# One decoder layer on one core: which weight granules the DMA queue splits, the order of the attention half of the output projection, and the division of SBUF between weight buffers and general slots

## The chip, the cores and the metric

The kernel runs on one core of a Trainium2 chip. The core has five engines, each with an instruction queue that is worked off in order: TensorE (PE; its weight loads are shown as PEld), VectorE (DVE), ScalarE (ACT), GpSimd (POOL) and SyncE (SP). SP and POOL also issue the transfers between HBM and SBUF. The metric is the device time of one execution in microseconds (us); lower is better.

## The reference

One layer works on x of 512 positions by 1024 channels, in float32. What matters here:

```python
h = rms_norm(x, norm1_g[l])
proj = h @ w_in[l]
z, xbc, dt, q, kv, gates = jnp.split(proj, split_points, axis=-1)
y_ssm = ssd_mixer(z, xbc, dt, ...)
y_nsa = rms_norm(nsa_mixer(q, kv, gates, ...), attn_norm_g[l])
x = x + jnp.concatenate([y_ssm, y_nsa], axis=-1) @ w_out[l]
h = rms_norm(x, norm2_g[l])
u = causal_dwconv(h @ ffn_w_up[l], ffn_conv_w[l], ffn_conv_b[l])
ug, uv = jnp.split(u, 2, axis=-1)
x = x + (jax.nn.silu(ug) * uv) @ ffn_w_down[l]
return rms_norm(x, final_norm_g)
```

`ssd_mixer` is a state-space scan in four chunks of 128 positions. `nsa_mixer` is an attention with a compressed, a selected and a windowed branch; the compressed branch first makes 31 compressed keys and values out of windows of 32 positions.

## The kernel before

**Products in three parts.** Every large product is made of three matmuls: each operand is split into a rounded part (high) and the rest (low), and high by high, high by low and low by high are added in one PSUM bank. So each weight granule (128 partitions by 1024 columns, 512 KB) is needed as `wh` (high) and `wl` (low).

**Two ways to split a granule.** The 144 granules are consumed in a fixed sequence `seq`: 0 to 39 of w_in, 40 to 55 of w_out (40 to 47 for the attention half, 48 to 55 for the scan half), then the feed-forward part. `by_dma(i)` picks the way. By the engines: two transfers of 256 KB from SP's queue into slots `wr`, then for each half ACT (or DVE, as CAST) writes `wh`, and DVE or POOL subtracts to make `wl`. By DMA: POOL issues one transfer of 512 KB into `wh`, ACT writes its negated rounded value into `wl`, and POOL issues a second transfer of the same 512 KB that adds the granule onto `wl`; the granule is thus read from HBM twice, and neither DVE nor POOL computes.

**Look-ahead and buffers.** `w_get(i, ahead)` hands out granule i and records the splits of the following ones (two, or three when the next is split by DMA) and the loads of two more (LOOK). There are 7 buffers `wh` and 7 `wl`; all other tiles of 2 KB a partition share 53 slots.

**The planner sets the order.** The program is first recorded and then placed by `schedule`, a list scheduler with its own costs: at each step the engine that can start earliest takes the ready operation that was recorded first. It also picks the engine (ACT or DVE, DVE or POOL) and the buffer. The order of every engine's queue is therefore an outcome of the recorded order, of the costs (among them the rate it assumes for a transfer, 360, or 180 for an adding one) and of the free buffers.

**The stages on PE, in order.** `first_job` (granules 0 to 3, tiles `psa`, while the norm's row sums are made: `n1ss`, `n1rb`, then hT, the normalised and transposed input, in `hTh` and `hTl`); the compressed branch's projections (4 to 7, `psb`), whose results are copied by SP transfers into shifted tiles `x2a` and `x2b`, gathered into `cxb` by ACT and DVE and multiplied in `compress` (tile `cps`); keys, queries and the scan's inputs (8 to 39) woven with the attention (`pss`, `tb`, `o`); then the scan `ssd` woven with `out_nsa` (40 to 47, tiles `on`); `out_ssm` (48 to 55, tiles `os`); the second norm (`n2`, `tb`) and the feed-forward part (`psb`, `dn`).

**out_nsa before.** For each half of the 1024 output columns it fetches its four granules at once, loads x again into `xr`, and then takes one block of 128 positions (t) after the other: 24 matmuls over all four granules into one bank `on`, then a DVE operation that scales the bank and adds it to `xr`. `out_ssm` goes t by t over four granules in the same way.

Of the kernel before, what the change touches and what calls it, by code (L numbers as in the profile page):

```python
# [15 lines left out]
ALU = mybir.AluOpType  # L16
# [5 lines left out]
NT = 4  # L22
# [1 line left out]
KC = 8  # L24
FF = 2816
NEG = -1.0e30
N_SLOT = 53
N_WH = 7
N_WL = 7
AHEAD = 3  # L30
LOOK = 2
D0, D1 = 8, 56
N_EAGER = 3
HEADS = (4, 2, 1, 1)
N_WARM = 10
# [133 lines left out]
class Program:  # L169
# [82 lines left out]
    def _cost(self, op, e, n, args, kw, ins, outs):  # L252
# [12 lines left out]
            return ins[0].free / 1.2 + (52 if is_ps[0] else 94) + 93 * extra, TABLE.get(args[2].name, 0)  # L265
        if n == "dma_start" and e == "POOL":
            v = outs[0]
            op.lat = v.ids.shape[0] * v.free * 4 / (180.0 if "accum_op" in kw else 360.0)
            return 1000.0, 0
        if e in ("DVE", "POOL"):  # L270
            f = max([v.free for v in ins] + [outs[0].free])
# [14 lines left out]
                op.port[e] = e == "POOL" or sb > 1 or (sb == len(big) == 1 and not is_ps[0] and n not in ("reciprocal", "tensor_reduce"))  # L286
            return cost * (2.0 if e == "POOL" else 1.0), 0
        v = (outs + ins)[0]
        op.lat = v.ids.shape[0] * v.free * 4 / 360.0
        return 650.0, 0  # L290


# [119 lines left out]
def layer_kernel(ctx: ExitStack, tc: tile.TileContext, x, xt, win, wdtg, wout, wup, wdn, pack, gcol, rows, cw1, consts, rot, out):  # L412
# [20 lines left out]
    def bank(name, shape=(P, T)):  # L433
        return alloc(pp, shape, F32, name, "b", 8)
# [238 lines left out]
    RS = {}  # L673
# [524 lines left out]
    def nsa_root(h):  # L1198
        ps = bank("oss", (P, 2, 2))
        for t in range(2):  # L1200
            for p_ in range(2):
                mm(ps[:, t], ACC[h][:, p_, t], ones[:, 0:2], start=p_ == 0, stop=p_ == 1)
        r = rstd_of(ps[:, :, 0], 2, 1024, 1e-6, "nsa")
        for t in range(2):
            RS["nsa", 2 * h + t] = r[:, t:t + 1]
# [47 lines left out]
    def nxt(n=1):  # L1253
        g = gi[0]
        gi[0] += n
        return g
# [124 lines left out]
    X1 = {}  # L1381

    def out_nsa(half):
        if half == 0:
            for h in range(2):
                for g in range(4):
                    if g >= N_EAGER:
                        nsa_ops(g, h)
                nsa_root(h)
        for t in range(NT):  # L1390
            X1[t, half] = slot(f"xr{t}")
            SP.dma_start(X1[t, half], x[t * P:(t + 1) * P, half * 512:(half + 1) * 512])
        g0 = nxt(4)
        ws = [w_get(g0 + p_, 3 - p_) for p_ in range(4)]
        for t in range(NT):
            ps = bank(f"on{t}")
            for p_ in range(4):
                for j in range(2):
                    tri(ps, mix(t, 2 * p_ + j), [a[:, j * 512:(j + 1) * 512] for a in ws[p_]],
                        p_ == 0 and j == 0, p_ == 3 and j == 1)  # L1400
                yield 1.3
            V.scalar_tensor_tensor(X1[t, half], ps, RS["nsa", t], X1[t, half], op0=ALU.mult, op1=ALU.add)

    def out_ssm(half):
        g0 = nxt(4)
# [205 lines left out]
```

## Time and profile before

| | |
|---|---|
| time, median of 3 runs | 919.08 us (918.53 to 921.29) |
| the profiled execution: time, and its span from first to last instruction | 917.42 us, 915.6 us |
| PE busy in the span | 883.9 us (97%) |
| DVE busy | 682.8 us (75%) |
| ACT busy | 433.0 us (47%) |
| POOL busy | 111.0 us (12%) |
| bytes moved by transfers | 106.02 MB |
| granted TensorE clock, mean | 0.994 |

Busy is the time in which an engine had an instruction running; matmuls overlap each other, so a busy PE is not PE at its peak. A matmul of 512 columns shows a duration of some 390 ns, yet follows the one ahead of it after 0.23 us when nothing is waited for. All times below are counted from the start of the span.

### The profile page before, as it was taken

What the parts mean: (1) busy time and instruction counts of PE and PEld (TensorE: products, weight loads), DVE (VectorE), ACT (ScalarE), POOL (GpSimd) and SP (SyncE); (2) the same over time, 40 slices, a digit from 0 to 9 for tenths busy, and PEclk for the clock granted to TensorE, in tenths of its full rate; (3) what the DMA queues carried; (4) which work ended last, traced back from release to release, by engine and by line L of the source; (5) the groups of instructions that cost most, each with busy time, mean ns of one, the idle gap of its engine ahead of it and who ended that gap; (6) DMA issues with size and microseconds to landing.
All of it is one profiled execution on the core that took longest, in us unless ns stands there. A gap on an engine that the chain in (4) does not pass through costs nothing.

```text
span 915.6 us, 13236 instructions
## 1 busy us (share of the span) xinstructions
PE 883.9 (97%) x4621; PEld 727.6 (79%) x4621; DVE 682.8 (75%) x1466; ACT 433.0 (47%) x939; POOL 111.0 (12%) x138
## 2 busy tenths in 40 slices
PE   8998999999999999999999999999999999999996
PEld 5776777787887799888777779888888888888885
DVE  6956899998889876689898477777773347777535
ACT  5624577787676666578665244222321113222113
POOL 0331231111111111102322221000000000000000
PEclk9999999999999999999999999999999999999999
DMA  8798754454454454432859922111112661000002
GB/s 274 222 223 204 168 119 96 95 121 106 103 127 93 93 105 103 93 116 48 209 165 304 332 83 93 54 50 47 47 58 98 227 226 35 1 0 1 1 1 92
DMA packets 45217, 106.02 MB, mean 116 GB/s; under 512 B 5984, under 2 KB 6752, under 8 KB 45152
## 3 DMA queue, kind: packets, MB, share of 16 engines
q0 software_dynamic: 13824, 50.34, 24.6%
q1 hardware_dynamic: 31328, 54.86, 18.3%
q8 instruction: 36, 0.59, 0.3%
q14 instruction: 29, 0.24, 0.1%
HBM read 97.31 MB, written 2.10 MB: 109 GB/s over the span
## 4 chain that ended last, share of the span: by engine, by line
PE 74%; DVE 10%; DMA 6%; issue 6%; ACT 2%; POOL 2%; SPq 1%; POOLq 0%; DVEq 0%; ACTq 0%
PE psb L400 36%; PE dn L400 13%; PE psa L400 8%; PE pss L400 5%; PE tb L400 4%; PE o L400 4%; PE os L400 2%; DMA rw<-rx 1%; DMA x2b<-rx 1%; PE on L400 1%; DVE hTl L400 1%; DMA wl<-in_wout_dram 1%; DMA x2b<-vcr 1%; SPq L400 1%; DMA wr<-in_win_dram 1%
## 5 line engine op out<-in xcount | busy, mean ns | idle before, releaser
L400 PE MATMUL psb<-hTh,wh 128*128 128x512 f32 (+1 forms) x600 | 232.8, 390 | 2.5 <-ACT cup L400 1.0
L400 PE MATMUL psb<-hTl,wh 128*128 128x512 f32 (+1 forms) x600 | 230.4, 384 | 2.3 <-DVE hTl L400 2.3
L400 PE MATMUL psb<-hTh,wl 128*128 128x512 f32 (+1 forms) x600 | 230.0, 384 | 0.0
L400 ACT ACTIVATE wh<-wr 128x512 fp32r<-128x512 f32 x80 | 49.8, 631 | 202.0 <-PE psb L400 102.1
L400 PEld LDWEIGHTS psb<-hTh,wh 128*128 128x128 f32 x600 | 113.2, 189 | 23.7 <-ACT cup L400 1.5
L400 PEld LDWEIGHTS psb<-hTl,wh 128*128 128x128 f32 x600 | 113.3, 189 | 23.5 <-DVE hTl L400 3.6
L400 PEld LDWEIGHTS psb<-hTh,wl 128*128 128x128 f32 x600 | 113.2, 189 | 21.6
L400 DVE TENSOR_TENSOR wl<-wr,wh 128x512 fp32r<-128x512 f32 x133 | 90.2, 714 | 17.1 <-ACT wh L400 16.8
L400 DVE CAST wh<-wr 128x512 fp32r<-128x512 f32 x68 | 28.9, 426 | 91.9 <-PE psb L400 43.7
L400 ACT ACTIVATE p<-pss,nm 128x128 f32<-128x128 f32 (+3 forms) x128 | 66.8, 525 | 38.0 <-DVE nm L400 21.3
L400 PE MATMUL dn<-wh,gTh 128*128 128x512 f32 (+1 forms) x186 | 70.3, 378 | 0.0
L400 PE MATMUL dn<-wl,gTh 128*128 128x512 f32 (+1 forms) x186 | 70.3, 378 | 0.0
L400 PE MATMUL dn<-wh,gTl 128*128 128x512 f32 (+1 forms) x186 | 70.2, 378 | 0.0
L400 DVE TENSOR_TENSOR ptl<-tb,pth 128x512 fp32r<-128x512 f32 x80 | 54.3, 687 | 14.6 <-ACT pth L400 11.0
L400 ACT ACTIVATE wl<-wh 128x1024 fp32r<-128x1024 f32 x48 | 50.6, 1056 | 27.7 <-DMA wh<-in_wout_dram 14.9
L400 DVE TENSOR_REDUCE nm<-pss 128x1 f32<-128x384 f32 (+3 forms) x88 | 55.5, 633 | 4.0 <-PE pss L400 3.4
L400 PE MATMUL tb<-ck,p 128*128 128x128 f32 x320 | 51.4, 275 | 1.4 <-DVE p L400 1.0
L400 POOL TENSOR_TENSOR wl<-wr,wh 128x512 fp32r<-128x512 f32 x15 | 21.0, 1410 | 225.6 <-ACT wh L400 206.2
L400 ACT ACTIVATE pth<-tb 128x512 fp32r<-128x512 f32 x62 | 36.9, 598 | 21.9 <-PE tb L400 16.4
L400 POOL DMA_DIRECT2D wl<-in_win_dram x32 | 28.2, 882 | 150.4 <-ACT wl L400 136.3
L400 PEld LDWEIGHTS tb<-ck,p 128*128 128x128 f32 x320 | 37.5, 140 | 8.8 <-DVE p L400 1.2
L400 PEld LDWEIGHTS dn<-wh,gTh 128*128 128x128 f32 x186 | 35.0, 188 | 6.7 <-DVE xr L400 0.2
(325 smaller groups left out, 1739.2 us busy)
## 6 DMA issues: line engine op xcount, KB each, us to landing
wr<-in_wup_dram SPq DMA_DIRECT2D x88, 256.0 KB, 4.3
wh<-in_win_dram POOLq DMA_DIRECT2D x32, 512.0 KB, 4.1
wl<-in_win_dram POOLq DMA_DIRECT2D x32, 512.0 KB, 5.4
wr<-in_wdn_dram SPq DMA_DIRECT2D x44, 256.0 KB, 3.4
wh<-in_wout_dram POOLq DMA_DIRECT2D x16, 512.0 KB, 5.3
wl<-in_wout_dram POOLq DMA_DIRECT2D x16, 512.0 KB, 7.5
wr<-in_win_dram SPq DMA_DIRECT2D x16, 256.0 KB, 7.0
rw<-rx SPq DMA_DIRECT2D x56, 64.0 KB, 3.8
```

The costliest lines, as they stand in the source:

```text
L400: getattr(engines[op.eng], name)(*[real(a) for a in args], **{k: real(v) for k, v in kw.items()})
```

## The change

Four things change. The granules split by DMA are 16 to 47 instead of 8 to 55: granules 8 to 15 and 48 to 55 now go through `wr` and are split by the engines. There are 5 buffers `wh` and 5 `wl` instead of 7 and 7, and 61 slots instead of 53 (the same SBUF in all). `out_nsa` takes granule by granule: each granule's six matmuls for each of the four t go into four banks that stay open over the four granules, x is loaded again after that in the recorded order, and the four banks are read at the end. And the planner assumes lower transfer rates (290 and 145).

```diff
-N_SLOT = 53
-N_WH = 7
-N_WL = 7
+N_SLOT = 61
+N_WH = 5
+N_WL = 5
 AHEAD = 3
 LOOK = 2
-D0, D1 = 8, 56
+D0, D1 = 16, 48
...
-            op.lat = v.ids.shape[0] * v.free * 4 / (180.0 if "accum_op" in kw else 360.0)
+            op.lat = v.ids.shape[0] * v.free * 4 / (145.0 if "accum_op" in kw else 290.0)
...
-        op.lat = v.ids.shape[0] * v.free * 4 / 360.0
+        op.lat = v.ids.shape[0] * v.free * 4 / 290.0
...
+        ps = [bank(f"on{t}") for t in range(NT)]
+        g0 = nxt(4)
+        for p_ in range(4):
+            w = w_get(g0 + p_)
+            for t in range(NT):
+                for j in range(2):
+                    tri(ps[t], mix(t, 2 * p_ + j), [a[:, j * 512:(j + 1) * 512] for a in w],
+                        p_ == 0 and j == 0, p_ == 3 and j == 1)
+                yield 1.3
         for t in range(NT):
             X1[t, half] = slot(f"xr{t}")
             SP.dma_start(X1[t, half], x[t * P:(t + 1) * P, half * 512:(half + 1) * 512])
-        g0 = nxt(4)
-        ws = [w_get(g0 + p_, 3 - p_) for p_ in range(4)]
         for t in range(NT):
-            ps = bank(f"on{t}")
-            for p_ in range(4):
-                for j in range(2):
-                    tri(ps, mix(t, 2 * p_ + j), [a[:, j * 512:(j + 1) * 512] for a in ws[p_]],
-                        p_ == 0 and j == 0, p_ == 3 and j == 1)
-                yield 1.3
-            V.scalar_tensor_tensor(X1[t, half], ps, RS["nsa", t], X1[t, half], op0=ALU.mult, op1=ALU.add)
+            V.scalar_tensor_tensor(X1[t, half], ps[t], RS["nsa", t], X1[t, half], op0=ALU.mult, op1=ALU.add)
```

Since the planner decides, the order moves at many places. Three of them bear on what follows.

PE, before, at the end of `first_job` (`n1rb` spreads the norm's factor over the partitions, `psa` are the first granules' products, `psb` the first product that needs hT):

```order
L400 MATMUL n1rb_384<-ck_128,n1r_363 128x128 x4
L400 MATMUL psa_130<-wh3_231,xgh_238 128x512
L400 MATMUL psa_134<-wh3_231,xgh_238 128x512
L400 MATMUL psa_119<-wl3_253,xgh_238 128x512
L400 MATMUL psa_123<-wl3_253,xgh_238 128x512
L400 MATMUL psa_130<-wl3_253,xgh_238 128x512
L400 MATMUL psa_134<-wl3_253,xgh_238 128x512
L400 MATMUL psa_119<-wh3_231,xgl_310 128x512
L400 MATMUL psa_123<-wh3_231,xgl_310 128x512
L400 MATMUL psa_130<-wh3_231,xgl_310 128x512
L400 MATMUL psa_134<-wh3_231,xgl_310 128x512
L400 MATMUL psb_419<-hTh_405,wh4_316 128x512
```

PE, the change, at the same place:

```order
L400 MATMUL psa_129<-wl3_264,xgh_261 128x512
L400 MATMUL psa_135<-wl3_264,xgh_261 128x512
L400 MATMUL psa_119<-wh3_253,xgl_299 128x512
L400 MATMUL psa_125<-wh3_253,xgl_299 128x512
L400 MATMUL psa_129<-wh3_253,xgl_299 128x512
L400 MATMUL psa_135<-wh3_253,xgl_299 128x512
L400 MATMUL n1rb_414<-ck_123,n1r_357 128x128 x4
L400 MATMUL psb_451<-hTh_447,wh4_341 128x512
L400 MATMUL psb_453<-hTh_447,wh5_366 128x512
L400 MATMUL psb_459<-hTh_447,wh6_388 128x512
```

Before, ten `psa` matmuls stand between `n1rb` and the first product that needs hT; in the change they stand ahead of `n1rb`, and none is left behind it. On DVE, meanwhile, six subtractions `wl` (granules 4 to 6) now stand between the small operations that make the norm's factor `n1r`.

PE, before, at the first matmuls of the compressed branch (`cps`; `psb_665` is granule 8 and `psb_740` granule 9, of which 24 and 18 matmuls stand ahead of `cps`):

```order
L400 MATMUL psb_740<-hTh_405,wl9_345 128x512
L400 MATMUL psb_740<-hTh_405,wh9_269 128x512
L400 MATMUL psb_740<-hTl_417,wh9_269 128x512
L400 MATMUL psb_740<-hTh_405,wl9_345 128x512
L400 MATMUL cps_795<-cxb_722,cwk0_321 128x130 x3
L400 MATMUL cps_795<-cxb_725,cwk0_321 128x130
L400 MATMUL cps_795<-cxb_725,cwk1_331 128x130 x2
L400 MATMUL cps_795<-cxb_729,cwk1_331 128x130 x2
L400 MATMUL psb_740<-hTh_405,wh9_269 128x512
L400 MATMUL psb_740<-hTl_417,wh9_269 128x512
```

PE, the change, at the same place (`psb_710` is granule 8, `dtgT` the transposes of the gates):

```order
L400 MATMUL psb_710<-hTh_447,wh8_487 128x512
L400 MATMUL psb_710<-hTl_455,wh8_487 128x512
L400 MATMUL psb_710<-hTh_447,wl8_544 128x512
L400 MATMUL psb_710<-hTh_447,wh8_487 128x512
L400 MATMUL psb_710<-hTl_455,wh8_487 128x512
L400 MATMUL psb_710<-hTh_447,wl8_544 128x512
L400 MATMUL cps_729<-cxb_656,cwk0_309 128x130 x2
L400 MATMUL dtgT_736<-ck_123,dtg_712 128x64 x4
L400 MATMUL cps_729<-cxb_656,cwk0_309 128x130
L400 MATMUL psb_710<-hTh_447,wh8_487 128x512
L400 MATMUL psb_710<-hTl_455,wh8_487 128x512
L400 MATMUL psb_710<-hTh_447,wl8_544 128x512
```

The first `cps` now stands behind 6 matmuls of granule 8 instead of 42 of granules 8 and 9: PE comes to it 36 matmuls earlier. Ahead of the `x2a` and `x2b` copies in SP's queue there are now 14 more loads `wr` (granules 8 to 14), and POOL's first weight transfer is that of granule 16, where it was that of granule 8, issued at the very start.

POOL, before, at the end of the scan (granules 51 to 53):

```order
L400 TENSOR_TENSOR Cl_5525<-xbc_3356,Ch_5450 128x128
L400 TENSOR_TENSOR Cl_5550<-xbc_3442,Ch_5474 128x128
L400 TENSOR_TENSOR xsd_5459<-xsd_5459,hp_241 128x512
L400 DMA wh51_5593<-in_wout_dram 128x1024
L400 DMA wh52_5639<-in_wout_dram 128x1024
L400 DMA wl51_5661<-in_wout_dram 128x1024
L400 DMA wh53_5694<-in_wout_dram 128x1024
L400 DMA wh54_5717<-in_wout_dram 128x1024
L400 DMA wl52_5700<-in_wout_dram 128x1024
L400 DMA wl53_5793<-in_wout_dram 128x1024
```

POOL, the change, at the same place:

```order
L400 TENSOR_TENSOR Cl_5526<-xbc_3353,Ch_5500 128x128
L400 TENSOR_TENSOR Cl_5587<-xbc_3469,Ch_5513 128x128
L400 TENSOR_TENSOR xsd_5568<-xsd_5568,hp_232 128x512
L400 TENSOR_TENSOR pvl_5721<-prev_5498,pvh_5563 128x512
L400 TENSOR_TENSOR wl50_5734<-wr_5187,wh50_5471 128x512
L400 TENSOR_TENSOR wl50_5734<-wr_5190,wh50_5471 128x512
L400 TENSOR_TENSOR wl51_5831<-wr_5232,wh51_5709 128x512
L400 TENSOR_TENSOR wl52_5852<-wr_5441,wh52_5773 128x512
L400 TENSOR_TENSOR wl52_5852<-wr_5449,wh52_5773 128x512
```

The transfers of these granules are gone from POOL, and five of the subtractions of granules 50 to 52 have taken their place (a sixth, of granule 48, stands 12 rows further up); DVE has the other four halves of granules 48, 49 and 51, and all of 53 to 55. On SP the loads `wr` of granules 48 and 49 now stand ahead of the `xr` loads of the first half; the second half's `on` banks are opened on PE before those of the first half are read on DVE.

## Rows read from the trace of the kernel before

Columns of the timeline are: start, duration, engine, line, operation, written and read tiles, sizes, count, and in brackets the idle time ahead of it with what ended it.

**Rows 1.** The page, busy time of each engine (share of the span, instructions).

```profile
PE 883.9 (97%) x4621; PEld 727.6 (79%) x4621; DVE 682.8 (75%) x1466; ACT 433.0 (47%) x939; POOL 111.0 (12%) x138
```

**Rows 2.** The waits of PE: who waited for what, total, times, longest.

```profile
PE os L400 <- DMA wl<-in_wout_dram: 5.0, 2, 3.2
PE psa L400 <- ACT wh L400: 3.2, 1, 3.2
PE cps L400 <- issue: 3.1, 1, 3.1
PE psb L400 <- DVE hTl L400: 2.3, 3, 1.2
```

**Rows 3.** Windows: busy (count) of PE, PEld, DVE, ACT, POOL, clock, DMA share, GB/s.

```profile
70.00:80.00 10.00, 6.92 (x36) 5.83 (x35) 5.05 (x28) 3.28 (x10) 1.45 (x2) 0.92 1.07 252
...
490.00:500.00 10.00, 8.24 (x41) 6.50 (x40) 8.22 (x22) 3.25 (x7) 2.18 (x4) 1.00 1.02 305
...
520.00:530.00 10.00, 6.75 (x28) 5.21 (x27) 1.13 (x2) 0.60 (x1) 0.88 (x1) 0.95 0.82 251
...
540.00:550.00 10.00, 10.00 (x67) 9.02 (x67) 9.87 (x27) 6.44 (x13) 5.59 (x4) 1.00 0.53 173
...
450.00:475.00 25.00, 23.91 (x141) 19.00 (x140) 23.23 (x49) 15.45 (x40) 6.53 (x7) 1.00 0.62 174
...
575.00:600.00 25.00, 25.00 (x112) 20.71 (x111) 19.18 (x32) 7.77 (x12) 0.00 (x0) 1.00 0.13 43
```

**Rows 4.** The timeline of PE in the second half of the scan's output projection.

```profile
528.73 0.65 PE L400 MATMUL os<-wl,hTh 128*128 128x512 f32 x1 [3.25 <-DMA wl<-in_wout_dram]
529.18 0.63 PE L400 MATMUL os<-wh,hTl 128*128 128x512 f32 x1
...
532.17 0.48 PE L400 MATMUL os<-wl,hTh 128*128 128x512 f32 x1
```

**Rows 5.** The timeline of PE at the compressed branch.

```profile
77.11 2.64 PE L400 MATMUL cps<-cxb,cwk 128*128 128x130 f32 x16 [3.08 <-issue]
...
79.97 0.63 PE L400 MATMUL psb<-hTl,wh 128*128 128x512 f32 x1
...
81.68 0.44 PE L400 MATMUL psb<-hTh,wl 128*128 128x512 f32 x1
```

**Rows 6.** The timeline of SP's transfers ahead of it.

```profile
69.80 1.10 SPq L400 DMA_DIRECT2D x2b<-rx  x2
```

**Rows 7.** The timeline of PE at the start.

```profile
8.85 2.08 PE L400 MATMUL psa<-wh,xgh 128*128 128x512 f32 x4 [3.21 <-ACT wh L400]
...
31.91 1.05 PE L400 MATMUL n1rb<-ck,n1r 128*128 128x128 f32 x8
...
35.10 0.84 PE L400 MATMUL psb<-hTh,wh 128*128 128x512 f32 x3
```

**Rows 8.** The timeline of DVE while hT is made.

```profile
33.00 2.06 DVE L400 SCALAR_TENSOR_TENSOR xT<-xT,gT,n1rb 128x512 f32<-128x512 f32 x3 [0.66 <-PE n1rb L400]
...
45.97 2.38 DVE L400 TENSOR_TENSOR hTl<-xT,hTh 128x512 fp32r<-128x512 f32 x1
```

**Rows 9.** The timeline of POOL at the same time.

```profile
46.21 1.58 POOL L400 TENSOR_TENSOR wl<-wr,wh 128x512 fp32r<-128x512 f32 x1
```

**Rows 10.** The page, costliest groups: busy us, mean ns of one, idle before.

```profile
L400 ACT ACTIVATE wh<-wr 128x512 fp32r<-128x512 f32 x80 | 49.8, 631 | 202.0 <-PE psb L400 102.1
...
L400 DVE TENSOR_TENSOR wl<-wr,wh 128x512 fp32r<-128x512 f32 x133 | 90.2, 714 | 17.1 <-ACT wh L400 16.8
...
L400 POOL TENSOR_TENSOR wl<-wr,wh 128x512 fp32r<-128x512 f32 x15 | 21.0, 1410 | 225.6 <-ACT wh L400 206.2
```

**Rows 11.** Transfers: count, size of one, median us from issue to landing.

```profile
wr<-in_wup_dram SPq DMA_DIRECT2D x88, 256.0 KB, 4.3
...
wr<-in_win_dram SPq DMA_DIRECT2D x16, 256.0 KB, 7.0
...
xr<-in_x_dram SPq DMA_DIRECT2D x8, 256.0 KB, 6.9
```

## The prediction

> **What bounds the kernel now.** Read the busy times first [rows 1]: PE has an instruction running in 883.9 of 915.6 us. A kernel like that can only become faster in the 31.7 us in which PE has nothing, or where PE runs slowly. So the second view is the list of PE's waits [rows 2]: each row says what PE waited for, in total, how often, and the longest one. Its largest entry is the one the change touches most directly: `os`, the scan half of the output projection, waits 5.0 us in two pieces for `wl` of w_out, the adding transfer. Behind it stand the first product (3.2 us), the compressed branch (`cps`, 3.1 us) and hT (2.3 us). Third, the windows [rows 3] say what the DMA engines did at these places: a share of 1.02 from 490 to 500, 0.82 from 520 to 530 and 1.07 from 70 to 80, that is, full or nearly so; where the feed-forward part runs undisturbed it is 0.13, and 112 matmuls of 512 columns take 25.0 us, 0.223 us each. The waits of PE thus stand where granules split by DMA, each read twice, crowd the queue. What a wait costs is more than its length, by the timelines: after the 3.25 us wait of `os` the next eight matmuls start from 528.73 to 532.17, 0.43 us apart, half the rate [rows 4]; after the 3.08 us wait of `cps` the four from 79.97 to 81.68 also [rows 5].
>
> The sum is made against the profiled execution (917.42 us, of which 1.8 lie outside the span). It stands 1.66 us below the median of the runs, 919.08, so the same difference is taken off that.
>
> **Part 1: granules 48 to 55, split by the engines.** Removed: the two waits for `wl`, 5.0 us [rows 2], and the slow matmuls behind the longer, 3.44 us in place of 8 x 0.223 = 1.78, so 1.7 us [rows 4]: **-6.7**. Added for each granule: two halves of 0.63 us on ACT and two of 0.71 on DVE or 1.41 on POOL [rows 10], loads of 256 KB whose median is 4.3 us where the queue is free and 7.0 where it is full [rows 11]. What covers it: the loads no longer need a `wh` buffer but slots, and stand far ahead. The buffers are the tight point. Four granules are held through a half of `os`, so with five buffers granule 53 can be split only when 48 has had its last use. From then to the first use of 53 lie 24 matmuls of 0.223 us, 5.4 us; the split takes 0.63 + 2 x 0.71 = 2.1 us and some handing over. So it is hidden with 3 us to spare; without that cover each of three granules would cost its 2.1 us, 6.3 in all. Taken: -6.7, bounds -6.7 and -0.4.
>
> **Part 2: the compressed branch.** Before, the last `x2b` copies were issued at 69.80, took 1.10 us to issue alone [rows 6], and `cps` came at 77.11 [rows 5]. With granules 8 to 15 read once, 4 MB less crosses the DMA engines in the first 100 us, and POOL has no weight transfer there at all. But the planner has moved `cps` forward by 36 matmuls, 36 x 0.223 = 8.0 us, as the order shows: PE, which came to it at 77.11 - 3.08 = 74.0, now comes at 66.0. The wait goes only if the copies land 11.1 us earlier. They cannot be issued before the rotated keys are there. I estimate that 6 to 11 us of this is gained by an empty queue (copies that land in some 4 us, the low row of the transfers [rows 11], and not 7, twice in a row, since the rotation has a transfer of its own). So a new wait of 0 to 5 us stands at 66, against the old 3.1 plus about 1 us of slow matmuls [rows 5]. Taken: a wait of 1.5, and **-2.6**; bounds -4.1 and +2.6 (a wait of 5 and 1.7 of slow matmuls behind it). The extra splits here (14 halves, 0.71 us on DVE or 1.41 on POOL each, rows 10) lie in a stretch where DVE is busy 5.05 of 10 us [rows 3].
>
> **Part 3: the start.** The first product waits 3.21 us for granule 0 [rows 7]. In the change the two transfers of 512 KB that POOL issued at the start are gone, so granule 0 should land nearer to 4.3 us than to 7.0 [rows 11]: up to -2.7. Against it: ten `psa` matmuls, 2.2 us, no longer cover the way from `n1rb` to the first product with hT (31.91 to 35.10 before, rows 7), and six subtractions of 0.71 us, 4.3 us, stand inside the chain that makes `n1r`. hT itself is DVE work, eight scalings of 0.69 (three in 2.06) and eight subtractions [rows 8], that neither edit shortens. Taken: **-0.5**, bounds -2.7 and +4.3.
>
> **Part 4: the scan stage.** DVE is busy 23.23 of 25 us there, PE 23.91 [rows 3], so both are near full. Counting instructions by kind in the order, DVE has the same work up to the last chunk within 1 us: three subtractions more, two `xdl` and two readings of `on` fewer. POOL has six subtractions of 1.41 us more and sixteen DMA issues fewer. A POOL subtraction slows DVE: `hTl` took 2.38 us at 45.97 [rows 8] while POOL subtracted for 1.58 us [rows 9], against 0.71 for a DVE subtraction. Five of the six come when the scan is almost over, where PE has the first half of `os` to do. The x loads of `out_nsa`'s first half are a second cost: they now come late, a load took 6.9 us [rows 11], and DVE's in-order queue stands behind the reading of the banks until they land. Taken: **+2.0** for both; bounds 0 and +8.5 (6 x 1.41, every POOL subtraction at DVE's full cost).
>
> The Trainium skill has a rule for that upper bound (SBUF — State Buffer, section "SBUF: two separate sides"): VectorE with two SBUF inputs and a GpSimd operation that reads SBUF exclude each other, and the second fully blocks until the first has ended. The trace agrees, with `hTl` longer by 1.67 us beside a POOL subtraction of 1.58. By that rule alone part 4 would come to +8.5.
>
> **Part 5: into the feed-forward part.** With 7 buffers granules 56 to 58 were split under `os`; now 57 to 59 come into the stretch of the second norm, where DVE is busy 9.87 of 10 us [rows 3]. Two to three halves more there: **+0.5**, bounds 0 and +2.1 (3 x 0.71). Elsewhere (the attention, granules 16 to 39) operations and costs are those of before; with four granules ahead, each used for some 10 us, the look-ahead is still long. Lower planner rates only reorder there: 0.
>
> **Sum.** -6.7 - 2.6 - 0.5 + 2.0 + 0.5 = -7.3: 910.1 for a profiled execution, **911.8** for the median.
>
> **Rivals.**
> - *Only the output projection gains.* The new wait at `cps` is as long as the old one and the start gives nothing: -6.7 + 2.5 = -4.2, so 914.9. For it speaks that the planner put `cps` forward by as much as it believed in; against it the DMA share of 1.07 that goes.
> - *All parts come well.* No wait at `cps` (-4.1), the first product 2.7 earlier, the scan stage at +0.5: -13, so 906.
> - *POOL shuts DVE out.* Part 4 at its +8.5 while parts 2 and 3 give little (-1): -6.7 - 1 + 8.5 + 0.5 = +1.3, so 920.4, no change. For it: DVE at 23 of 25 us has no slack to take it [rows 3]. Against it: where the five subtractions stand.
> - *Banks run short: slower.* Four banks stay open for `on`, and the second half opens more before the first is read; the scan's own tiles, about 17 bank uses a chunk in four chunks, have to go through what is left. If each use waited 0.3 us for its bank, 68 x 0.3 = 20 us would be added in the stage: 919.1 - 9.3 (the sum without part 4) + 20 = 930. It decides from 0.15 us a use on, where the gain is gone. For it: PE works in order, so each such wait stops the covering `on` matmuls too. Against it: among PE's waits [rows 2] none of the larger is for a bank.
>
> **How the numbers follow.** A measurement of this kernel tells a change of 0.3% (2.8 us) from none: below 916.3 is faster, above 921.8 slower. Chances: the forecast (908.5 to 913.5) 0.42, only the output projection (913.5 to 916.3) 0.22, all well (below 908.5) 0.12, no change 0.14, slower 0.10. Faster 0.76, same 0.14, slower 0.10. The range, 905 to 918.5, leaves out the slower case, some of no change and the lowest end of the best. Where it is faster, 906 to 916 holds it.
>
> **What the profile after would show.** Part 1: no row "PE os <- DMA wl" among PE's waits, and clock 1.00 from the last `on` to `psb`; wrong if `os` waits for ACT, DVE or POOL's `wl`. Part 2: `cps` near 66 to 68; wrong if its wait is over 4 us or longer than before. Part 3: the first `psa` at 6 to 7 us, and a wait of some 2 us before the first `psb`. Part 4: the stretch from the first scan matmul to the last `on` as long as before within 3 us; wrong if `xr` rows on DVE wait long for "DMA xr", or `seg`, `yd` or `xst` wait for engines that free a bank. Part 5: `tb` of the second norm waiting no more than a microsecond longer. The forecast falls if the attention stage itself, which I set to 0, comes out different by more than 2 us.

## The result, and the profile after

| | before | after |
|---|---|---|
| median of the runs | 918.81 us (917.98 to 921.29, 4 runs) | 907.66 us (907.25 to 908.01, 4 runs) |
| span of the profiled execution | 915.6 us | 906.2 us |
| mean granted clock | 0.994 | 0.993 |

The ratio is 0.9874, with an interval of 0.9854 to 0.9894 that lies wholly below 1: the change is faster by 11.2 us, or 1.3%. Forecast were 911.8 and a gain of 7.3.

The busy times on the page of the changed kernel answer to [rows 1]: PE 5.1 us less, POOL 17.7 less, DVE 13.9 more.

```profile
PE 878.8 (97%) x4621; PEld 725.3 (80%) x4621; DVE 696.7 (77%) x1478; ACT 439.4 (48%) x972; POOL 93.3 (10%) x109
```

Its waits of PE (total, times, longest) answer to [rows 2]. The two largest entries of before, `os` for `wl` and the first product, are gone, and so is `cps`. At the top stand waits for `p` and hT, and `os` waits for DVE's `t`.

```profile
PE tb L400 <- ACT p L400: 3.3, 2, 3.0
PE psb L400 <- ACT hTh L400: 2.8, 1, 2.8
PE psb L400 <- DVE hTl L400: 2.8, 3, 1.9
PE os L400 <- DVE t L400: 2.5, 1, 2.5
...
PE tb L400 <- DVE yg L400: 1.0, 1, 1.0
```

Windows of the changed kernel (columns as in [rows 3]): from 70 to 80 PE is full and the DMA share is 0.18 where it was 1.07. From 110 to 120, where PE was full before, it is busy 5.99 of 10 us, at a clock of 0.74, while DVE is full.

```profile
70.00:80.00 10.00, 10.00 (x47) 7.94 (x46) 9.59 (x35) 3.96 (x14) 0.73 (x1) 1.00 0.18 54
110.00:120.00 10.00, 5.99 (x28) 3.96 (x26) 9.88 (x22) 7.67 (x25) 4.03 (x5) 0.74 0.39 75
450.00:475.00 25.00, 24.30 (x156) 19.79 (x155) 24.44 (x54) 19.07 (x52) 6.59 (x9) 1.00 0.54 168
490.00:500.00 10.00, 9.20 (x44) 7.43 (x45) 8.85 (x26) 2.53 (x6) 0.00 (x0) 1.00 0.88 274
520.00:530.00 10.00, 10.00 (x51) 8.15 (x50) 8.78 (x26) 2.30 (x6) 0.00 (x0) 1.00 0.01 2
```

**Where the time went.** Since the order of PE differs everywhere, stages are compared at equal work. For each shape of matmul I took the shortest usual interval to the next start (the 10th percentile in the profile before). Added over all 4621 matmuls that is 797.5 us, the same for every kernel here. What a kernel has taken beyond that, when so much of the work is done, is its loss. The columns are stretches of this work: 0 to 15 (first products), to 40 (first norm, hT), to 90 (with the compressed branch), to 130 (first attention tiles), to 350 (attention, which ends at about 320, and the first chunk of the scan), to 398 (the other chunks, `out_nsa`, the first `os`), to 445 (rest of `os`, second norm), and the rest. The short names are those of the experiments below. The table compares single profiled executions: before and after lie 9.4 us apart in it, where the medians lie 11.2 apart. The profiled execution of e8 was the longest of its twelve.

```
                     0-15   -40   -90  -130  -350  -398  -445  rest   total lost
before                7.0   4.8  11.8  11.6  49.2  14.0   9.9   9.8   118.2
after                 2.4  10.8   4.9  16.9  45.6  14.6   3.6  10.0   108.8
after - before       -4.6  +6.0  -7.0  +5.3  -3.6  +0.6  -6.3  +0.2    -9.4

e1  range to 55       2.0  11.1   5.0  17.2  45.6  12.9  19.8   9.6   123.2
e2  range from 8      6.9   6.1   9.4  16.0  46.1  14.7   3.6  10.0   112.8
e3  old order         1.4  10.9   5.3  16.7  46.8  16.0   3.9  10.0   111.0
e4  factor first      2.0   4.2   5.1  16.3  45.4  14.8   3.6  10.0   101.3
e5  subs on DVE       2.2   9.4   4.8  17.2  45.6  12.0   3.2  10.0   104.4
e6  e4 and e5         2.4   4.0   5.4  16.8  46.3  12.2   3.2   9.9   100.5
e7  old buffers       2.3   3.9   9.5  16.9  46.8  14.1   5.8   9.7   109.1
e8  old rates         1.6  14.5   5.9  18.4  46.7  17.2   4.0   9.9   118.2
e9  range alone       2.2  10.8   5.4  18.0  48.1  22.2   3.5   9.9   120.1
e10 order alone       7.3   4.5  11.9  11.9  48.3  11.9   4.5   9.8   110.1
e11 rates alone       7.6   3.0   9.5  17.8  46.7  12.9   9.6  10.1   117.2
e12 order, rates      6.3   3.1   9.5  18.9  46.4  11.8  10.8  10.2   116.9
```

### The profile page after: what moved, and what is told of

Its sections match the earlier page's. It is cut to its first block, busy times and chain, and to the rows that moved or that the text cites. A ratio compares the mean times of both kernels' runs of the same rounds, so it can differ in the third digit from the quotient of the medians.

```text
span 906.2 us, 13305 instructions
## 1 busy us (share of the span) xinstructions
PE 878.8 (97%) x4621; PEld 725.3 (80%) x4621; DVE 696.7 (77%) x1478; ACT 439.4 (48%) x972; POOL 93.3 (10%) x109
## 4 chain that ended last, share of the span: by engine, by line
PE 82%; DVE 10%; DMA 3%; ACT 2%; SPq 1%; issue 1%; DVEq 0%; ACTq 0%
PE psb L400 37%; PE dn L400 13%; PE psa L400 6%; PE tb L400 5%; PE os L400 5%; PE pss L400 5%; PE o L400 4%; PE on L400 4%; SPq L400 1%; PE yd L400 1%; DMA xT<-in_xt_dram 1%; DMA rw<-rx 1%; DVE wl L400 1%; DVE hTl L400 1%; DVE rx L400 1%
## 5 line engine op out<-in xcount | busy, mean ns | idle before, releaser
L400 ACT ACTIVATE wh<-wr 128x512 fp32r<-128x512 f32 x110 | 67.6, 631 | 218.8 <-PE psb L400 114.8
L400 DVE TENSOR_TENSOR wl<-wr,wh 128x512 fp32r<-128x512 f32 x164 | 109.4, 699 | 15.5 <-ACT wh L400 15.0
L400 DVE CAST wh<-wr 128x512 fp32r<-128x512 f32 x70 | 29.7, 425 | 92.3 <-PE psb L400 46.8
L400 ACT ACTIVATE pth<-tb 128x512 fp32r<-128x512 f32 x67 | 39.9, 597 | 24.8 <-PE tb L400 23.4
L400 PEld LDWEIGHTS dn<-wh,gTl 128*128 128x128 f32 x186 | 35.0, 188 | 6.5
L400 PEld LDWEIGHTS dn<-wl,gTh 128*128 128x128 f32 x186 | 35.0, 188 | 6.4
```

The lines of the kernel that those rows point to most:

```text
L400: getattr(engines[op.eng], name)(*[real(a) for a in args], **{k: real(v) for k, v in kw.items()})
```

## Experiments

Before was run on each chip beside them: 918.06 (e1 to e4), 917.78 (e5 to e8), 918.38 (e9, e10) and 917.81 (e11, e12). Differences between kernels are of their medians.

### e1: the scan half of the output projection split by DMA again

```diff
-D0, D1 = 16, 48
+D0, D1 = 16, 56
```

> The change with granules 48 to 55 split by DMA again (the rest as in the change); the order on PE is the same up to the scan stage. If the gain at the scan half of the output projection comes from its adding transfers being gone, their wait returns: PE waits for wl of w_out by 5 us or more (with five buffers granules 52 to 55 cannot even be loaded before 48 to 51 are let go, so up to 10 us), and the time is 914 to 921 us. If the gain came from the planner's new order or from the start, this run stays within 2 us of the change, 906 to 910.

Measured: 922.22 us (919.79 to 925.37), ratio 1.0054 (1.0037 to 1.007). Granules 48 to 55 thus decide 14.6 us of the changed kernel; the time is 1.2 above the range that was expected. In the table 16.2 more are lost between 398 and 445 and 1.7 less just ahead of it. The waits of PE show two places, and `os` is the smaller:

```profile
PE tb L400 <- DVE n2y L400: 7.9, 2, 4.5
...
PE os L400 <- DMA wl<-in_wout_dram: 2.6, 1, 2.6
```

The wait of `os` is the old one, but shorter than the 5 us that were expected. The larger is in the second norm, which was not expected, and a good part of it is POOL's. Its four subtractions of granules of the feed-forward part:

```profile
535.23 4.97 POOL L400 TENSOR_TENSOR wl<-wr,wh 128x512 fp32r<-128x512 f32 x4 [19.35 <-ACT wh L400]
```

and DVE's chain of tiny operations that makes the norm's factor at the same time, the first row from 2.6 us ahead of it:

```profile
532.64 0.22 DVE L400 SCALAR_TENSOR_TENSOR n2q<-n2r,n2u 128x1 f32<-128x1 f32 x1
...
536.58 1.19 DVE L400 SCALAR_TENSOR_TENSOR n2q<-n2r,n2u 128x1 f32<-128x1 f32 x1
537.70 0.14 DVE L400 TENSOR_SCALAR n2r<-n2u 128x1 int32<-128x1 int32 x1
...
538.92 1.29 DVE L400 SCALAR_TENSOR_TENSOR n2q<-n2r,n2u 128x1 f32<-128x1 f32 x1
```

An operation of 0.22 us takes 1.2 to 1.3 beside POOL. Four operations of the chain are held up so, by 4.1 us in all; DVE's own splits of a granule take another 1.9 out of it. This is read from the trace: no run kept POOL off this place. Before, POOL has four subtractions in the second norm as well (from 541.43), but the first `n2y` is out at 536.92, and PE doesn't wait. So the range up to 47 does two things in the changed kernel: it takes the transfers out from under `os`, and it has the engines' splits begin there and not inside the second norm.

### e2: granules 8 to 15 split by DMA again

```diff
-D0, D1 = 16, 48
+D0, D1 = 8, 48
```

> The change with granules 8 to 15 split by DMA again. If the early gain is the emptier queue, the first product starts near 8.9 us again instead of 5.7, PE waits 2 us or more for the compressed branch or comes to it at 74 us or later, and the time is 911 to 916 us. If the early gain is given back anyway (hT is ready no earlier, the attention waits for something else), the time is 907 to 910.

Measured: 911.32 us (909.41 to 912.37), ratio 0.9923 (0.9894 to 0.9952), 3.7 us above the changed kernel, as expected if the early gain is the emptier queue. The first product waits 3.3 us again and `cps` 2.4, and hT is made with less loss. In the first 90 us of work e2 loses 22.4, the changed kernel 18.1: the early range gains 4.5 at the first product and 4.5 around the compressed branch, and pays 4.7 of that at hT.

### e3: the old order of the attention half

`out_nsa` is that of before, all else changed. Some lines of it:

```diff
-        ps = [bank(f"on{t}") for t in range(NT)]
...
-            w = w_get(g0 + p_)
...
+        ws = [w_get(g0 + p_, 3 - p_) for p_ in range(4)]
         for t in range(NT):
+            ps = bank(f"on{t}")
```

> The change with the attention half of the output projection in its old order (four granules held, one t after the other, x loaded first). If that order as such is worth nothing, 906.5 to 909.5 us. The rival is that with five buffers the granule order is what lets the granules 48 to 52 be split in time: then os waits for ACT, DVE or POOL by 3 us or more and the time is 911 us or above. If the four open banks and the late loading of x cost something, the time is below 906.5.

Measured: 910.16 us (908.62 to 913.71), ratio 0.992 (0.9898 to 0.9943): the order is worth 2.5 us here. That lies between the two ranges that were expected.

### e4: the factor of the first norm ahead of six subtractions

Two edits of the changed kernel: the subtractions of granules 4 to 6 wait for the last operation of `n1r`, and their rounding stays on ACT.

```diff
-                S.activation(wh[i][:, cs], r, AF.Copy)
-                DP.tensor_sub(wl[i][:, cs], r, wh[i][:, cs].bitcast(F32))
+                top = S.activation(wh[i][:, cs], r, AF.Copy)
+                if 4 <= i <= 6:
+                    del top.alts["DVE"]
+                late = DP.tensor_sub(wl[i][:, cs], r, wh[i][:, cs].bitcast(F32))
+                if 4 <= i <= 6:
+                    held.append(late)
...
+    pr.order(factor[0], held)
```

> The change with the subtractions of granules 4 to 6 held until the norm's factor n1r is made, and their rounding kept on ACT. n1rb then has 11 psa matmuls behind it as before the change. If the six subtractions in the factor's chain and the missing cover cost what the trace of the change suggests (2.84 us wait for hTh at 33.95), hT is ready 3 us earlier and the time is 903.5 to 906.0 us. If hT's production on DVE bounds this stage anyway, or what is gained is given back before the attention, 906.5 to 908.5.

Measured: 902.44 us (900.54 to 904.12), ratio 0.9831 (0.9809 to 0.9853), 5.2 below the changed kernel and 1.1 below the range that was expected. The stretch from 15 to 40 loses 4.2 us and not 10.8; everything behind it stays. DVE's timeline of the changed kernel:

```profile
32.39 2.06 DVE L400 SCALAR_TENSOR_TENSOR xT<-xT,gT,n1rb 128x512 f32<-128x512 f32 x3
34.36 1.89 DVE L400 TENSOR_TENSOR hTl<-xT,hTh 128x512 fp32r<-128x512 f32 x3
36.17 1.40 DVE L400 SCALAR_TENSOR_TENSOR xT<-xT,gT,n1rb 128x512 f32<-128x512 f32 x2
37.49 2.65 DVE L400 CAST hTh<-xT 128x512 fp32r<-128x512 f32 x2
40.06 3.44 DVE L400 TENSOR_TENSOR hTl<-xT,hTh 128x512 fp32r<-128x512 f32 x2
```

In e4 the first scaling of hT starts at 28.68, 3.7 us earlier. The rows show a second piece: the two CASTs and two subtractions from 37.49 take 6.1 us where e4's first two of each take 0.75 + 1.28. POOL subtracts beside them, four times:

```profile
37.12 5.83 POOL L400 TENSOR_TENSOR wl<-wr,wh 128x512 fp32r<-128x512 f32 x4 [36.67 <-ACT wh L400]
```

e4 moves both. The trace of e2 helps to tell them apart: there too six subtractions stand in the chain of `n1r`, no `psa` is left behind `n1rb`, and PE waits 2.9 us for `hTh`; but POOL doesn't subtract beside hT (its first subtraction is at 50.27), hT's scalings and subtractions take 0.68 to 0.74 us each, and the stretch loses 6.1. So of the 6.0 that the changed kernel loses more than before, 1.3 are in e2 too, and 4.7 are not. Behind its wait of 2.8 us for `hTh` the changed kernel waits 0.4, 1.9 and 0.7 us more, between 38 and 44, beside POOL's four subtractions. This is a comparison of two kernels that differ in the granules 8 to 15 as well, so it sizes the two pieces only roughly.

### e5: three granules' subtractions kept off POOL; e6: both

The changed kernel with this; in e4's, whose subtraction is named `late` already, the last two lines alone:

```diff
-                DP.tensor_sub(wl[i][:, cs], r, wh[i][:, cs].bitcast(F32))
+                late = DP.tensor_sub(wl[i][:, cs], r, wh[i][:, cs].bitcast(F32))
+                if 50 <= i < 53:
+                    del late.alts["POOL"]
```

> The changed kernel, but the subtractions that make the low halves of granules 50 to 52 may not be given to POOL; DVE does them. In the changed kernel POOL does five of them from 482.06 to 489.60, and DVE's small operations of that stretch, 0.15 us elsewhere, take 0.67 to 1.02; PE waits 2.45 us (os for DVE's t) and 1.03 us (tb for DVE's yg). Theory POOL shuts DVE out: the small operations are back at 0.15 to 0.2 us, the t that frees the bank for os ends some 2 to 3 us earlier, the two waits together fall from 3.5 to under 1.5 us, and the time from 907.7 to 904.5 to 906.5. Rival, DVE has too much to do there whoever subtracts: up to five subtractions of 0.69 us more stand in DVE's queue, the two waits stay at 3 us or grow, and the time is 907 to 910.

Measured: 903.51 us (903.48 to 903.62), ratio 0.9855 (0.9831 to 0.9878): 4.15 below the changed kernel, and 1.0 below the range that was expected. POOL in the changed kernel at the end of the scan:

```profile
482.06 2.54 POOL L400 TENSOR_TENSOR wl<-wr,wh 128x512 fp32r<-128x512 f32 x2
484.88 4.72 POOL L400 TENSOR_TENSOR wl<-wr,wh 128x512 fp32r<-128x512 f32 x3 [0.29 <-DMA wr<-in_wup_dram]
```

DVE beside it, and the first matmul of `os`, which needs the bank that `t` reads:

```profile
483.29 0.74 DVE L400 SCALAR_TENSOR_TENSOR xr<-on,nsar,xr 128x512 f32<-128x512 f32 x1
483.95 0.67 DVE L400 TENSOR_TENSOR ssdq<-ssdq,ssdu 128x2 f32<-128x2 f32 x1
...
485.14 1.02 DVE L400 SCALAR_TENSOR_TENSOR ssdr<-ssdq,ssdr 128x2 f32<-128x2 f32 x1
...
486.69 0.68 DVE L400 TENSOR_TENSOR t<-yo,eac 128x512 f32<-128x512 f32 x1
...
487.42 0.50 PE L400 MATMUL os<-wh,hTh 128*128 128x512 f32 x1 [2.45 <-DVE t L400]
```

The same in e5, where `t` comes 3.4 us earlier and `os` waits 0.43:

```profile
483.19 0.14 DVE L400 SCALAR_TENSOR_TENSOR ssdr<-ssdq,ssdr 128x2 f32<-128x2 f32 x1
483.26 0.68 DVE L400 TENSOR_TENSOR t<-yo,eac 128x512 f32<-128x512 f32 x1
...
483.99 0.50 PE L400 MATMUL os<-wh,hTh 128*128 128x512 f32 x1 [0.43 <-DVE t L400]
```

2.6 us of the gain lie in the column up to 398 and 0.4 behind it. Another 1.4 lie between 15 and 40, where the order of every engine is the same in both kernels and the longest wait for `hTl` was 1.0 and not 1.9; that is not where the edit works. That POOL shuts DVE out is shown; at this place it costs some 3 us.

> The kernel of e4 (factor of the first norm ahead of six subtractions) with the edit of e5 as well. The two places are 440 us apart. If both causes are right and independent, the gain of e5 over the changed kernel comes off e4's 902.4: 899.2 to 901.2. If DVE is simply overloaded at the end of the scan: 902 to 904.

Measured: 899.27 us (898.1 to 899.72), ratio 0.9806 (0.9782 to 0.9831). That is 3.2 below e4, so the two places are nearly independent, as expected; it is the fastest kernel here.

### e7 and e8: the old buffers, the old rates

```diff
-N_SLOT = 61
-N_WH = 5
-N_WL = 5
+N_SLOT = 53
+N_WH = 7
+N_WL = 7
```

> The changed kernel with the buffers of before: seven wh and seven wl, 53 general slots. Counted at equal work, PE loses 50.3 us between 110 and 350 us of matmul work in the changed kernel and 54.4 before, and the same 50 in the three kernels that undo the granule range or the order of the attention half: so this gain of 4 us must come from buffers, slots or the planner's rates. Theory slots: with 53 slots the attention stage loses 54 again, and the time is 910.5 to 913. Rival, the granule range alone carries all of it, and buffers only had to make it fit: 906.5 to 909.5. The second possibility on the slow side: too few slots for sixteen granule halves ahead at the end, waits of os or of the second norm, over 913.

Measured: 906.66 us (905.05 to 908.33), ratio 0.9886 (0.9862 to 0.9909). Beside the rest the buffers are worth nothing in the total. By the table they move losses about: 6.9 less at hT, 4.6 more around the compressed branch (`cps` waits 2.6 us) and 2.2 more between 398 and 445. The attention (130 to 350 in the table) loses 46.8 with 53 slots too, nearer to the 45.6 of the changed kernel than to the 49.2 of before; the theory of the slots fell.

```diff
-            op.lat = v.ids.shape[0] * v.free * 4 / (145.0 if "accum_op" in kw else 290.0)
+            op.lat = v.ids.shape[0] * v.free * 4 / (180.0 if "accum_op" in kw else 360.0)
...
-        op.lat = v.ids.shape[0] * v.free * 4 / 290.0
+        op.lat = v.ids.shape[0] * v.free * 4 / 360.0
```

> The changed kernel with the planner's transfer rates of before (360 and 180 in place of 290 and 145). Theory that rates only reorder: 906.5 to 909.5, with cps at 64 to 70 us and the attention stage's loss at 50 to 51 us. Theory that the slower rates give the attention stage its gain of 4 us, since the planner then leaves more room for loads: attention loses 54 again and the time is 910.5 to 913.

Measured: 911.74 us (909.26 to 917.47), ratio 0.9947 (0.9928 to 0.9966): the rates are worth 4.1 us. The time is that of the second theory, but not its place: from 170 to 437 us the granted clock is 1.00 in this execution too, and the attention loses 46.7, 2.5 below the 49.2 of before. The profiled execution was the longest of its twelve, at a mean clock of 0.982, so its other columns are not sized here.

### e9 to e12: parts alone on the kernel before

The edits of these four are pieces of the diff of the change, made on the kernel before. e9:

```diff
-N_SLOT = 53
-N_WH = 7
-N_WL = 7
+N_SLOT = 61
+N_WH = 5
+N_WL = 5
...
-D0, D1 = 8, 56
+D0, D1 = 16, 48
```

> The kernel before with the granule range 16 to 47 and the changed buffers (five and five, 61 general slots), but the old order of the attention half and the old transfer rates. Undoing the order costs the changed kernel 2.5 us and undoing the rates 4.1. Theory that the parts add: 907.7 + 2.5 + 4.1 = 914.3, so 913 to 916. Theory that the range carries nearly all and the two others only matter once both are there: 909 to 912. The wait of os for wl should be gone either way, and the cps wait under 1 us.

Measured: 920.67 us (919.32 to 922.95), ratio 1.0023 (1.0011 to 1.0036): no gain, 2.3 us slower, above both ranges that were expected. The wait of `os` is gone, as foreseen, but the attention half, which still holds four granules at once and now has five buffers, waits for the same kind of transfer:

```profile
PE on L400 <- DMA wl<-in_wout_dram: 3.2, 2, 1.9
```

The stretch from 350 to 398 loses 8.2 more than before. Beside these 3.2 us, PE waits there 5.4 us for what DVE makes for the scan (`sg`, `yg`, `pvl`).

e10 has the new `out_nsa` alone:

```diff
+        ps = [bank(f"on{t}") for t in range(NT)]
...
-        ws = [w_get(g0 + p_, 3 - p_) for p_ in range(4)]
...
+            w = w_get(g0 + p_)
...
```

> The kernel before with the new order of the attention half alone. Counted at equal work, the stretch between 350 and 390 us of matmul work loses 12.9 us before, 9.5 in the changed kernel and 12.7 there with the old order. Theory that the order itself gives that, whoever splits the granules: 914.5 to 916.5, with the waits of os for wl still there. Rival, the order only pays beside granules that the engines split, since granules that arrive by DMA, four of which it needs one after the other, make it wait: 917 to 921.

Measured: 910.03 us (908.62 to 912.7), ratio 0.9913 (0.9894 to 0.9932): 8.4 us from the order alone, well below both ranges that were expected. The surprise is that `os` doesn't wait for a transfer any more, though granules 48 to 55 come by DMA as before. POOL's issues of `wh` point to the reason. Before, granules 47 to 52:

```profile
436.22 0.59 POOL L400 DMA_DIRECT2D wh<-in_wout_dram  x1 [1.66 <-PE seg L400]
438.80 0.55 POOL L400 DMA_DIRECT2D wh<-in_wout_dram  x1 [1.99 <-PE yd L400]
441.31 0.53 POOL L400 DMA_DIRECT2D wh<-in_wout_dram  x1 [1.96 <-PE on L400]
445.66 0.55 POOL L400 DMA_DIRECT2D wh<-in_wout_dram  x1 [0.64 <-PE bt L400]
482.99 0.60 POOL L400 DMA_DIRECT2D wh<-in_wout_dram  x1 [1.22 <-PE seg L400]
485.84 0.53 POOL L400 DMA_DIRECT2D wh<-in_wout_dram  x1 [2.25 <-PE on L400]
```

In e10, granules 49 to 52:

```profile
433.79 0.56 POOL L400 DMA_DIRECT2D wh<-in_wout_dram  x1 [0.71 <-PE seg L400]
445.97 0.60 POOL L400 DMA_DIRECT2D wh<-in_wout_dram  x1 [1.66 <-PE bt L400]
456.83 0.59 POOL L400 DMA_DIRECT2D wh<-in_wout_dram  x1 [0.45 <-PE seg L400]
468.32 0.55 POOL L400 DMA_DIRECT2D wh<-in_wout_dram  x1 [3.37 <-PE bt L400]
```

Position by position, four granules are freed within 10 us and their followers are fetched in one crowd, with no `wh` for 37 us after it. Granule by granule, a buffer comes free every 11 to 12 us, and the transfers spread. The first of the two waits follows from this: it ends when the adding transfer of granule 51 has landed, at 499.08 before and at 473.99 in e10, long ahead of its use. The second, longer wait is for granule 55, which stands behind the crowd (landed at 528.69 before, 521.43 in e10). And the crowd by itself doesn't make the wait: e11 below has the same one (436.36 to 445.60, the next `wh` at 479.16), issues granule 51 3.8 us earlier than before, and `os` waits 0.2. So the DMA split as such doesn't make `os` wait; the time at which a buffer comes free for it decides, and the crowd makes that late.

e11 has the lower rates alone, e12 the lower rates and the new `out_nsa`:

```diff
-            op.lat = v.ids.shape[0] * v.free * 4 / (180.0 if "accum_op" in kw else 360.0)
+            op.lat = v.ids.shape[0] * v.free * 4 / (145.0 if "accum_op" in kw else 290.0)
...
-        op.lat = v.ids.shape[0] * v.free * 4 / 360.0
+        op.lat = v.ids.shape[0] * v.free * 4 / 290.0
```

> The kernel before with the lower transfer rates of the planner alone. With the new range and the old order they were worth 10.5 us (920.7 to 910.2), with the new range and the new order 4.1 (911.7 to 907.7). Theory that lower rates only help where the five buffers leave little room: 916 to 920 here. Theory that they help whatever the rest is, since the planner then puts the granules' transfers earlier: 908 to 914, with the wait of os for wl under 2 us.

Measured: 915.78 us (913.27 to 917.39), ratio 0.9978 (0.9959 to 0.9997): a small gain, between the two ranges that were expected.

> The kernel before with the new order of the attention half and the lower rates, but the old range 8 to 55 and the old buffers. If the range is what carries the change, this stays near the order alone: 909 to 912. If order and rates carry it and the range gives nothing of its own (it cost 2.3 alone, and 1.7 beside the new order at the old rates), this comes to 904 to 908, as fast as the changed kernel.

Measured: 917.06 us (915.79 to 918.01), ratio 0.9989 (0.9972 to 1.0007): no change, where each of the two alone is faster, and outside both ranges. Both of these kernels lose 9.6 to 10.8 us between 398 and 445, not to `os` but to the second norm (`n2y`), as e1 did; POOL subtracts beside the norm's chain in both. They also lose 6 to 7 us more than before between 90 and 130, where `cs` waits for DVE's `q`. The waits of PE in e12:

```profile
PE tb L400 <- DVE n2y L400: 5.6, 3, 3.4
PE cs L400 <- DVE q L400: 4.8, 2, 4.5
```

## Why the prediction was right, and where it was not

The three parts together, as ratios to before (the second row has the changed buffers too; its third entry is e8, its second e3):

```
                old order            new order
                old rates new rates  old rates new rates
range 8 to 55   1         0.9978     0.9913    0.9989
range 16 to 47  1.0023    0.992      0.9947    0.9874
```

No part has a worth of its own. By these ratios and 918 us, the range costs 2 or 3 us beside the old rates and gives 5 or 11 beside the new; the rates give 2 to 10 or cost 7. (e8's medians, not set against before, gave 4.1 for the rates; its runs spread by 8 us.) The forecast sized the places of the whole change. It came near in parts 1, 4 and 5 and missed part 2, part 3 and the attention; where it named the edit that does it, the table corrects it. By stretches, -6.3, -7.0, +1.4, +0.6 and +0.2 stand against the -6.7, -2.6, -0.5, +2.0 and +0.5 of the five parts, and +1.7 against nothing for the attention. They add to -9.4 against -7.3. That the total came within about 2 us is in part luck: the 4.4 us that part 2 gave beyond its forecast and the 3.6 of the later attention stand against the 5.3 that the first attention tiles lost and the 1.9 that part 3 missed.

**Part 1** (-6.7). Measured between 398 and 445: -6.3. `os` has no wait for `wl`, and the granted clock is 1.00 from 490 to 500 and from 520 to 530. Size and place were right, the reason was half right: e9 shows that splitting by engines removes this wait, e10 that the order removes it as well, and e11 that the rates do, but for 0.2 us. What the prediction didn't see is that the split alone hands the wait on to `on` (e9), and that without it the second norm would pay under the new rates (e11, e12, e1).

**Part 2** (-2.6, with a new wait of 1.5). The new wait at `cps` didn't come; it starts at 66.56 without one, and the stretch from 40 to 90 gains 7.0, more than the bound of 4.1. So the copies landed earlier than was estimated. The next stretch loses 5.3 more than before. There PE stands 2.95 us before the first attention tiles that need `p`, and then runs at a granted clock of 0.50 to 0.52 from 114.6 to 120, the lower of the two levels (1.2 GHz):

```profile
114.61 1.35 PE L400 MATMUL tb<-ck,p 128*128 128x128 f32 x4 [2.95 <-ACT p L400]
```

It is tempting to call this the stall of `cps`, given back 48 us later. The runs speak against it. In e4 PE comes to the same place 6.9 us earlier and waits as long as in the changed kernel:

```profile
107.75 1.35 PE L400 MATMUL tb<-ck,p 128*128 128x128 f32 x4 [2.96 <-ACT p L400]
```

What differs from before is the order. From the first `pss` to this `tb` it takes 18.4 us before and 19.0 in the changed kernel, but 49 matmuls of 512 columns stand between them before and 36 now: 13 x 0.223 us, 2.9 us of cover, are gone. The range alone (e9) and the rates alone (e11) each bring such a loss (18.0 and 17.8 in this stretch, against 11.6 before), e11 with 4 matmuls of cover and its longest wait at `cs`; the order of `out_nsa` alone doesn't (e10, 11.9). So the step that failed is not in part 2 but in "lower planner rates only reorder there: 0": the reordering itself costs here. No run put the 13 matmuls back by themselves.

**Part 3** (-0.5). The first product gained 4.6, more than the bound of 2.7, since the prediction counted the wait alone. Behind it, before, the matmuls from 8.85 [rows 7] to 13.29 start 0.43 us apart, which the prediction counted behind `os` and `cps` but not here; after the change they start 0.23 apart. That is ten times 0.2, some 2 us. The second group of four before, and the same group after the change:

```profile
10.72 1.91 PE L400 MATMUL psa<-wl,xgh 128*128 128x512 f32 x4
```

```profile
6.74 1.07 PE L400 MATMUL psa<-wl,xgh 128*128 128x512 f32 x4
```

The hT chain lost 6.0: +1.4 together, inside the bounds. The lost cover and the six subtractions were rightly named as the danger. But the larger piece, by the comparison of e2 under e4, is POOL's subtracting beside hT, which the prediction knew from [rows 8] and [rows 9] and put into part 4 alone. e4 gets it all back, and 0.6 more.

**Part 4** (+2.0). Measured between 350 and 398: +0.6. From 350 to 390 the changed kernel loses 9.5 us where before loses 12.9 (the numbers of the expectation of e10; 12.7 with the old order), so the new order gains there, which was not foreseen; alone it gains 2.1 up to 398 (e10). The last 8 us of work lose some 4 more, and POOL's five subtractions are 2.6 of that (e5). The prediction counted on the first half of `os` as cover for them; but the first `os` itself waited, 2.45 us. DVE shows no wait for the x loads that come late. The Trainium skill (SBUF — State Buffer, section "SBUF: two separate sides") says that the second of a VectorE operation with two SBUF inputs and a GpSimd operation that reads SBUF waits until the first ends. The trace agrees, operation by operation: 0.15 becomes 0.67 and 1.02, and the two end at 484.62 and 486.16, where POOL's subtractions end at 484.60 and 486.15. The price of five times 1.41 is not reached; from 480 to 485 PE was busy 4.97 us with other work.

**Part 5** (+0.5): +0.2.

**The attention** was set to 0, and the prediction had said that it falls if this differs by over 2 us. Its first tiles lost 5.3 (under part 2) and the rest gained 3.6, 3.0 of it ahead of 320, where the attention ends. This is the step that failed outright, twice and in opposite directions. Of the gain, a third is idle time: PE's goes from 2.70 to 1.44 us between 130 and 390. The rest shows as no wait, and the granted clock is 1.00 in both: matmuls follow each other more closely. Of single edits, the rates alone give 2.5 of it (e11), range and order about 1 each (e9, e10); but range, buffers and order without the rates give 2.5 as well (e8), and no single edit undone takes away more than 1.2 (e1, e2, e3, e7, e8). So no part owns this gain, and by what way it comes stays open.

**The rivals.** "Only the output projection gains" comes true in sum for the first 130 us of work, whose four columns sum to -0.3, but by gains and losses that cancel, and not because nothing moved; it missed the later attention. "POOL shuts DVE out" was a true mechanism with less than its full price. "Banks run short" did not occur where it was looked for: from 399 to 487.3 the longest wait of PE is 0.6 us, for `sg`. One wait for a bank comes right after, the 2.45 us of the first `os` at 487.42, for the bank that DVE's `t` was late to read.

## What to carry to other kernels

Where a planner orders the program, undo each part and also try each alone: here the same part was worth a gain or a loss, depending on the others, and where one wait went, others came elsewhere (at `on` in e9, in the second norm in e11 and e12). An order that a planner chooses can cost by itself: count the matmuls that cover a chain, before and after. Buffers that come free together make transfers that crowd together; look at the times of issue before blaming the transfer's kind. Work handed to POOL to relieve DVE belongs where DVE has no chain that PE waits for: keeping three granules' subtractions off it gave 4.2 us (e5) and 3.2 (e6).

## What the runs showed of the hardware

- Beside a POOL operation of two inputs only some DVE operations are held up. In the changed kernel `hTl<-xT,hTh`, with both inputs in SBUF, has a median of 1.76 us (2 of them) against 0.68 alone (6); `xr<-on,nsar,xr`, whose input `on` is a PSUM bank, takes 0.74 beside POOL (6) and alone (2). Operations on one input aren't all alike: the TENSOR_SCALAR `n2r<-n2u` stays at 0.14 (537.70 in e1), `ssdu<-ssdu` goes from 0.15 alone (8) to 0.41 beside POOL's multiplications `xsd` and `xdt` (3), and two CASTs from SBUF took 2.65 beside its subtractions. It can be POOL that is held up: in e7 one of its subtractions takes 3.52 us from 37.18 on, and not 1.3, while DVE's `hTl` run beside it at 0.68.
- After a wait PE may go on at the lower level of its clock. In e1, behind the wait of 2.56 us of `os`, the granted clock is 0.50 from 514.5 to 517 (1.2 GHz), and matmuls start 0.43 us apart:

```profile
514.57 0.63 PE L400 MATMUL os<-wh,hTh 128*128 128x512 f32 x1
514.99 0.63 PE L400 MATMUL os<-wl,hTh 128*128 128x512 f32 x1
515.42 0.63 PE L400 MATMUL os<-wh,hTl 128*128 128x512 f32 x1
```

A wait of 2.45 us in the changed kernel (487.42) was not followed by this: the granted clock stays at 1.00 from 487.4 to 490, and the matmuls behind it start 0.23 us apart.
